# A transformer layer on one core: sums spread over the second sweep, and a written order for the passage into the second FFN

## The chip, the core and the metric

The kernel runs on one core of a Trainium2 chip. The core has five engines that run side by side and wait for each other through semaphores: TensorE (PE; its weight loads are shown apart as PEld), VectorE (DVE), ScalarE (ACT), GpSimd (POOL) and SyncE (SP), whose queue issues nearly all transfers here. TensorE writes to PSUM; the other data lies in SBUF or in the chip's main memory. The metric is the device time of one execution in microseconds (us), taken as the median of the runs.

## The reference, cut to what matters

One layer on 512 tokens of width 1024, all in float32. The weights are of the sizes in the comments.

```python
def swiglu(u, w_in, w_out):                      # w_in 1024 x 5632, w_out 2816 x 1024
    a, b = jnp.split(u @ w_in, 2, axis=-1)
    return (jax.nn.silu(a) * b) @ w_out

sh1, sc1, g1, sh2, sc2, g2, sh3, sc3, g3 = split(silu(c) @ w_ada + b_ada, 9)
u = rms_norm(x, ffn1_norm_g) * (1 + sc1) + sh1
x = x + 0.5 * g1 * swiglu(u, ffn1_w_in, ffn1_w_out)
u = rms_norm(x, mix_norm_g) * (1 + sc2) + sh2
z = u @ w_mix + b_mix                            # the mixer: an mLSTM branch and an attention branch
...
merged = sigmoid(g_a) * (y_a @ w_branch_a) + sigmoid(g_b) * (y_b @ w_branch_b)
x = x + g2 * (merged @ w_out)                    # w_out 1024 x 1024
u = rms_norm(x, ffn2_norm_g) * (1 + sc3) + sh3
x = x + 0.5 * g3 * swiglu(u, ffn2_w_in, ffn2_w_out)
```

## The kernel before, in words

**Products.** To keep float32 accuracy with the faster reduced format (`F32R`), each operand is split in a high half (`wh`, `uh`, `mh`, a rounded copy, made by ScalarE) and a low half (`wl`, `ul`, `ml`, what remains, made by VectorE as source minus copy). A product is three matmuls (`mm3`, lines 127 to 129): high by high, and each high by the other's low. A 512 KB piece of a weight goes through three steps: a transfer into one of three raw buffers (`raw`, line 92), the copy (line 102) and the subtraction (line 104), into one of four pairs of buffers `wh`, `wl`. The subtraction frees the raw buffer, TensorE's last use frees the pair.

**Order.** Each engine works through its instructions in a fixed order. A planner draws it up when the kernel is built, from a cost model: it takes what is ready by that model, what stands first in the program first. An instruction that is pinned (`keep_in_program_order`) stays behind the instruction of its engine that comes before it in the program. `self.pin` is either that function or one that does nothing (`self.free`). Later instructions that are not pinned may still be put between pinned ones. Transfers on the sync queue are issued in the planner's order, each after its waits.

**Output products of the two FFNs** (`pair_out`, from line 526). The 22 blocks of the hidden width are taken in 11 pairs, and the four 256-token by 512-column quarters of the output come from seven block products in place of eight, with sums of weights (`ws`, prepared earlier and kept in main memory) and of activations (`A1`, `A2`). The first sweep over the pairs makes three of the products (Z, X, Y); from them come P1, U2 and U4, each for two blocks of 128 tokens. The second sweep makes the other four (Z, Y, X, W, of two token blocks each, eight PSUM banks) in 8 iterations of 24 matmuls, two raw loads an iteration (`prepare`: c, the plain weights, and d, the sums). The last three iterations (the tail) are done bank by bank in the order X, Z, Y, W (`close`), so that sums and stores can run behind them. In iterations 3, 5 and 7 the d of a tail iteration is loaded ahead (`early`); in iterations 3 to 6 a block of x is loaded. At iterations 6 and 7, P1, U2 and U4 are multiplied by the gate g (`scaled`, line 597) and added to x (`onto`, line 600), seven operations an iteration. In the first FFN the tail is handed to `end` (written out in `run`, all pinned), which goes over into the mixer; the second FFN ends the kernel, with stores at line 607.

**Passage into the second FFN.** `token_gemm` (line 650) multiplies the merged branches with `w_out`: for each half of the columns, four PSUM banks (one for each block of 128 tokens), the weights in four pieces, the first piece for all blocks, the last three block by block. `done` (from `residual`) multiplies the bank by the gate, adds it to x and has ScalarE take the squares and their sum (`x_sq`). In the second column half, ahead of block 3's last pieces, `norm_half(0)` norms blocks 0 and 1: `xnorm` (a chain of small VectorE operations, then xn on VectorE and ScalarE), `norm_turn` (16 transposes on TensorE into four banks) and `norm_u` (for each k of 8: `uh` on ScalarE, `uf` on VectorE, and `ul`, the difference, on VectorE for even k and GpSimd for odd k, line 267). `norm_half(1)` does blocks 2 and 3 behind block 3. `ffn_in_halves` then makes the first two column tiles of both halves of `w_in` (four weight tiles) in halves of 256 tokens, tile after tile, with SiLU and product behind each pair. None of it is pinned. Then `ffn_in` takes the other 20 tiles, in 512-column matmuls, while weight sums for the output product are loaded (`sa`, `sb`) and made.

Of the kernel before, what the change touches and what calls it, by code (L numbers as in the profile page):

```python
# [11 lines left out]
F32 = mybir.dt.float32  # L12
# [35 lines left out]
class Layer:  # L48
# [209 lines left out]
    def u_from(self, ps, k, c0, w, G, sh, pool):  # L258

        nc = self.nc  # L260
        uf = self.tmp(pool, "uf")
        nc.scalar.activation(self.uh[k][:, c0:c0 + w], ps, AF.Identity, scale=G, bias=sh)
        if self.uf_act:
            nc.scalar.activation(uf[:, :w], ps, AF.Identity, scale=G, bias=sh)
        else:
            nc.vector.tensor_scalar(uf[:, :w], ps, G, sh, op0=MUL, op1=ADD)
        (nc.gpsimd if k % 2 else nc.vector).tensor_tensor(  # L267
            self.ul[k][:, c0:c0 + w], uf[:, :w], self.uh[k][:, c0:c0 + w], op=SUB)

# [12 lines left out]
    def norm_half(self, hf, pool, G, sh):  # L282

        xn = self.xnorm(hf, pool)
        self.norm_u(hf, self.norm_turn(hf, xn), pool, G, sh)

# [11 lines left out]

    def norm_u(self, hf, b, pool, G, sh):
        for k in range(NK):  # L300
            self.u_from(b[k // 2][:, k % 2 * 256:(k % 2 + 1) * 256], k, hf * 256, 256, G[:, k:k + 1], sh[:, k:k + 1], pool)
# [109 lines left out]

    def ffn_in_halves(self, w_in, nj, hp, tp):

        wa = [self.w_stat(w_in, j * P) for j in range(nj)]
        wb = [self.w_stat(w_in, FF + j * P) for j in range(nj)]
        pp = [(self.gbank(), self.gbank()) for _ in range(nj)]
        for h in range(2):
            for j in range(nj):
                c0, c1 = h * 256, (h + 1) * 256
                self.gemm_stat(pp[j][0], wa[j], c0, c1)  # L420
                self.gemm_stat(pp[j][1], wb[j], c0, c1)
                self.pair_h(self.pair_s(pp[j][0], c0, c1, tp), pp[j][1], j, c0, c1, hp, tp)


# [102 lines left out]
    def pair_out(self, w, v, hp, tp, x_src, end=None):  # L527
# [7 lines left out]
        def two(*src):  # L535

            n = 2 // len(src)
            t = self.raw(sh, [(lambda t, i=i: t[:, i:i + n, :] if n > 1 else t[:, i, :], a) for i, a in enumerate(src)])
            return self.split(t, sh)
        def early(src, n):  # L540

            hi, lo = [hp.tile(sh, F32R, name=self.nm("we"), tag=f"A{n + i}", bufs=1) for i in range(2)]
            t = lo.bitcast(F32)
            nc.sync.dma_start(t, src)
            nc.scalar.activation(hi, t, AF.Copy)
            V(lo, t, hi, op=SUB)
            return hi, lo
# [60 lines left out]
        tail, ds = 3, []  # L608
        for i in range(NP - tail):
# [39 lines left out]

    def token_gemm(self, lhs, nk, w, half, done, tail=2, extra=None, last=None):  # L650
# [18 lines left out]
        for tb in range(NT):  # L669
            if last and tb == NT - 1:  # L670
                last()
# [4 lines left out]
    def residual(self, factor, v, half, tp, final=False):  # L676
# [3 lines left out]
        def done(tb, half, ps):  # L680
            s = slice(half * 512, (half + 1) * 512)
            t = self.tmp(tp, "rs")
            nc.vector.scalar_tensor_tensor(t, ps, factor, g, op0=MUL, op1=MUL)
            x = self.x[tb][half]
            nc.vector.tensor_tensor(x, x, t, op=ADD)
            if not final:
                self.x_sq(tb, half, t)
            else:
                nc.sync.dma_start(self.out[0, tb * P:(tb + 1) * P, s], x)
# [592 lines left out]
    def run(self):  # L1282
# [7 lines left out]
        self.ntmp, self.xn_tiles, self.gb_tag, self.uf_act = 4, self.xn_ffn, ("gb", 2), True  # L1290
# [130 lines left out]
        self.uf_act = False  # L1421
# [75 lines left out]
        with tc.tile_pool(name="br", bufs=1) as bp:  # L1497
# [30 lines left out]
            def x_spill(h):  # L1528
                for tb in range(NT):
# [10 lines left out]
        with tc.tile_pool(name="f2t", bufs=1) as tp, tc.tile_pool(name="f2h", bufs=1) as hp:  # L1540
# [3 lines left out]
            self.ffn_in_halves(A["ffn2_w_in"][0], 2, hp, tp)  # L1544
# [44 lines left out]
```

## Time and profile before

| | |
|---|---|
| median of 3 runs | 1325.62 us (1324.99 to 1326.6) |
| the profiled execution | 1324.8 us |
| its span, first to last instruction | 1323.0 us |
| TensorE busy in the span | 1304.9 us (99%) |
| VectorE / ScalarE / GpSimd busy | 958.1 / 624.2 / 43.7 us |
| granted TensorE clock, mean | 0.999 |

The profile is of one execution. Its page gives the busy time of each engine; further views list who waited for whom, the instructions in order of time, and the busy time in given windows. Times in them count from the start of the span. A row of a timeline reads: start, duration, engine, line and operation, the tile written, the tiles read, the shape, and in brackets the engine's idle time before it with what ended it. A busy TensorE is not one at its peak, because matmuls overlap: a gap is read from the distance between starts.

### The profile page before, as it was taken

How to read it: one execution, taken by the hardware profiler on the slowest of the kernel's cores; microseconds unless marked ns; L12 is line 12 of the kernel's file. 1: busy time of each engine (PE TensorE's matmuls, PEld its weight loads, DVE VectorE, ACT ScalarE, POOL GpSimd, SP SyncE). 2: the span in 40 equal slices, each digit the busy share in tenths (PEclk: the TensorE clock that was granted, in tenths of full speed). 3: DMA queues.
4: the chain of work that ended last, by engine and by line, in shares of the span. 5: the costliest groups of instructions: out<-in, count | busy, mean ns of one | idle time of the engine just before them, and what ended most of it. 6: DMA issues, size and time to landing. Idle time of an engine off the chain costs nothing.

```text
span 1323.0 us, 17767 instructions
## 1 busy us (share of the span) xinstructions
PE 1304.9 (99%) x6332; PEld 1091.7 (83%) x6332; DVE 958.1 (72%) x1740; ACT 624.2 (47%) x1038; POOL 43.7 (3%) x65
## 2 busy tenths in 40 slices
PE   7999999999999999999999999999999999999998
PEld 6788888888799888888888788878888888888886
DVE  6877777477788687887877778777577656635777
ACT  5633233355476555566566666334262223223742
POOL 1000000000010101000000000003010000000000
PEclk9999999999999999999999999999999999999999
DMA  9999978465845434533243536777439777624574
GB/s 289 272 327 306 309 251 298 133 195 170 293 118 145 120 104 133 151 104 117 83 120 88 159 98 205 225 245 227 162 97 332 273 233 276 208 96 142 169 260 153
DMA packets 204344, 254.18 MB, mean 192 GB/s; under 512 B 14992, under 2 KB 146480, under 8 KB 204256
## 3 DMA queue, kind: packets, MB, share of 16 engines
q1 hardware_dynamic: 203872, 252.98, 60.0%
q8 instruction: 50, 0.82, 0.3%
q14 instruction: 38, 0.31, 0.1%
q0 software_dynamic: 320, 0.06, 0.0%
q10 hardware_dynamic: 64, 0.02, 0.0%
HBM read 217.28 MB, written 35.72 MB: 191 GB/s over the span
## 4 chain that ended last, share of the span: by engine, by line
PE 89%; DVE 4%; DMA 3%; ACT 2%; issue 1%; SPq 0%; POOL 0%; DVEq 0%; ACTq 0%; POOLq 0%
PE g L129 23%; PE g L127 23%; PE g L128 23%; PE t L128 4%; PE t L129 4%; PE t L127 4%; PE g L825 2%; PE t L1208 1%; PE t L1178 1%; DVE wl L104 1%; DMA x<-x_d 1%; PE t L1149 1%; PE t L825 1%; DMA raw<-in_ffn_w_out_dram 1%; PE t L1150 1%
## 5 line engine op out<-in xcount | busy, mean ns | idle before, releaser
L102 ACT ACTIVATE wh<-raw 128x1024 fp32r<-128x1024 f32 (+2 forms) x250 | 254.2, 1019 | 380.6 <-DMA raw<-in_ffn_w_in_dram 106.4
L104 DVE TENSOR_TENSOR wl<-raw,wh 128x1024 fp32r<-128x1024 f32 (+2 forms) x250 | 293.0, 1174 | 179.3 <-ACT wh L102 155.5
L128 PE MATMUL g<-ul,wh 128*128 128x512 f32 (+1 forms) x912 | 348.1, 383 | 1.1 <-POOL ul L267 1.1
L127 PE MATMUL g<-uh,wh 128*128 128x512 f32 (+1 forms) x912 | 348.7, 384 | 0.0
L129 PE MATMUL g<-uh,wl 128*128 128x512 f32 (+1 forms) x912 | 348.3, 382 | 0.0
L128 PEld LDWEIGHTS g<-ul,wh 128*128 128x128 f32 x912 | 171.3, 188 | 34.5 <-POOL ul L267 1.9
L129 PEld LDWEIGHTS g<-uh,wl 128*128 128x128 f32 x912 | 171.5, 188 | 33.6
L127 PEld LDWEIGHTS g<-uh,wh 128*128 128x128 f32 x912 | 171.0, 188 | 32.5 <-issue 0.6
L325 DVE SCALAR_TENSOR_TENSOR acc<-raw,ccol,acc 128x512 f32<-128x512 f32 (+1 forms) x70 | 66.8, 975 | 43.6 <-DMA raw<-in_w_ada_dram 43.5
L127 PE MATMUL g<-wh,uh 128*128 128x512 f32 (+1 forms) x256 | 97.4, 381 | 0.0
L129 PE MATMUL g<-wh,ul 128*128 128x512 f32 (+1 forms) x256 | 96.6, 378 | 0.0
L128 PE MATMUL g<-wl,uh 128*128 128x512 f32 (+1 forms) x256 | 96.4, 377 | 0.0
L128 PE MATMUL t<-wl,A 128*128 128x512 f32 x176 | 69.0, 392 | 1.7 <-DVE wl L104 1.7
L127 PE MATMUL t<-wh,A 128*128 128x512 f32 x176 | 68.6, 390 | 0.0
L129 PEld LDWEIGHTS g<-wh,ul 128*128 128x128 f32 x256 | 48.1, 188 | 9.0
L127 PEld LDWEIGHTS g<-wh,uh 128*128 128x128 f32 x256 | 48.2, 188 | 8.7 <-DVE tk L1046 0.5
L128 PEld LDWEIGHTS g<-wl,uh 128*128 128x128 f32 x256 | 48.2, 188 | 8.3
L129 PE MATMUL g<-yh,wl 128*128 128x512 f32 x128 | 50.1, 392 | 0.3 <-DVE wl L104 0.3
L127 PE MATMUL g<-yh,wh 128*128 128x512 f32 x128 | 49.8, 389 | 0.0
L128 PE MATMUL g<-yl,wh 128*128 128x512 f32 x128 | 49.8, 389 | 0.0
L455 ACT ACTIVATE A<-E 128x768 fp32r<-128x768 f32 x22 | 18.6, 846 | 57.0 <-DVE E L454 51.1
L1160 ACT ACTIVATE S<-S,mn 128x128 f32<-128x128 f32 (+1 forms) x64 | 35.6, 558 | 16.0 <-DVE mn L1152 9.9
(343 smaller groups left out, 2185.2 us busy)
## 6 DMA issues: line engine op xcount, KB each, us to landing
raw<-in_ffn_w_in_dram SPq DMA_DIRECT2D x82, 512.0 KB, 5.1
raw<-in_w_ada_dram SPq DMA_DIRECT2D x56, 512.0 KB, 5.5
raw<-in_w_mix_dram SPq DMA_DIRECT2D x46, 512.0 KB, 4.5
sa<-in_ffn_w_out_dram SPq DMA_DIRECT2D x22, 512.0 KB, 5.9
sb<-in_ffn_w_out_dram SPq DMA_DIRECT2D x44, 256.0 KB, 5.9
ws<-sa SPq DMA_DIRECT2D x22, 512.0 KB, 3.9
ws<-sb SPq DMA_DIRECT2D x44, 256.0 KB, 4.2
raw<-ws SPq DMA_DIRECT2D x44, 256.0 KB, 3.5
```

The lines of the kernel that those rows point to most:

```text
L102: nc.scalar.activation(hi, src, AF.Copy)
L104: self.last_lo = nc.vector.tensor_tensor(lo, src, hi, op=SUB)
L127: pin(mm(ps, lh, rh, start=start, stop=False))
L128: pin(mm(ps, lh, rl, start=False, stop=False))
L129: self.last_mm = pin(mm(ps, ll, rh, start=False, stop=stop))
L325: nc.vector.scalar_tensor_tensor(a, r[:, s], c, a, op0=MUL, op1=ADD)
L455: nc.scalar.activation(A1[:, 0:3, :], E[:, 0:3, :], AF.Copy)
L825: pin(nc.tensor.matmul(acc_ps[b], (wl if p == 1 else wh)[:, b % 2, s], self.ul[k] if p == 2 else self.uh[k], start=k == 0 and p == 0, stop ...
L1149: nc.tensor.matmul(ps[:, :w], q[:, s], k[:, :w], start=True, stop=False)
L1150: nc.tensor.matmul(ps[:, :w], q[:, s], kl[:, :w], start=False, stop=True)
L1160: nc.scalar.activation(S[:, ws], S[:, ws], AF.Exp, scale=-1.0, bias=m, accum_out=sm[:, qb:qb + 1])
L1178: tr = lambda b, c, qb, kb: nc.tensor.transpose(b[:, c:c + P], S[:, P_OFF[qb] + kb * P:P_OFF[qb] + (kb + 1) * P], self.ident)
```

## The change

In `pair_out` the three scalings of P1, U2 and U4 are done in place at iterations 0, 1 and 2 of the second sweep, and the additions to x, one block of tokens an iteration, at 4 to 7. In odd iterations the d weights are loaded into a tile of the tag `xn` in place of a raw buffer (`two_x`). In the second FFN the bank W of token block 1 is closed after iteration 7 and added to x; its last three iterations go into two new banks of 256 columns, each scaled, added and stored by itself.

The passage into the second FFN becomes one function, `passage`, that pins every engine's order. The second column half of the output product is the same, but the transposes stand behind the first three matmuls of block 3's last pieces. The weights of the first four FFN tiles are loaded and split in it, tiles 1 and 2 in two halves each into tiles of the tag `yl`. Both copies of u (`uh` and `uf`) are ScalarE's, and all subtractions VectorE's. TensorE takes tiles 0 and 1 together, k by k, then tile 2, the transposes of the second half, tile 3, and the second half in the same order. SiLU and product follow on whole 512-column banks. `norm_half`, `norm_u`, `u_from`, `ffn_in_halves` and `uf_act` are gone.

```diff
+        def two_x(src):
+            t = tp.tile(sh, F32, name=self.nm("raw"), tag="xn", bufs=1)
+            nc.sync.dma_start(t, src)
+            return self.split(t, sh)
...
-        banks = {"Z": Z, "Y": Y, "X": X, "W": W}
+        banks, tail = {"Z": Z, "Y": Y, "X": X, "W": W}, 3
         def prepare(i, d=None):
             c = two(both(2 * i + 1))
-            d = d or two(self.ws[i][:, 1:3, :])
+            d = d or (two_x if i % 2 else two)(self.ws[i][:, 1:3, :])
             A2 = self.A2[i]
             a = lambda n: (A2[0][:, n, :], A2[1 + n // 2][:, n % 2, :])
             b = lambda n: ((c, d)[n // 2][0][:, n % 2, :], (c, d)[n // 2][1][:, n % 2, :])
             return {"Z": (a(0), b(0)), "Y": (a(3), b(1)), "X": (a(2), b(2)), "W": (a(1), b(3))}
-        step = lambda n, tb, i, o: mm(banks[n], tb, *o[n], i == 0, i == NP - 1)
+        step = lambda n, tb, i, o: mm(banks[n], tb, *o[n], i == 0, i == NP - (1 if end or n != "W" or not tb else 1 + tail))
...
-        tail, ds = 3, []
+        ds = []
         for i in range(NP - tail):
...
-            if i in (6, 7):
-                tb = i - 6
-                add(P1[tb], 0, (tb,))
-                add(U2[tb], 0, (tb + 2,))
-                add(U4[tb], 1, (tb, tb + 2))
+            for src, half in ((P1, 0), (U2, 0), (U4, 1))[i:i + 1]:
+                for tb in range(2):
+                    scaled(src[tb], half, src[tb])
+            if i >= 4:
+                tb = i - 4
+                onto(tb, 0, (P1, U2)[tb // 2][tb % 2])
+                onto(tb, 1, U4[tb % 2])
...
+        add(W[1], 0, (3,))
         for n in "XZYW":
             for tb in range(2):
+                if n == "W" and tb:
+                    for c in (slice(0, 256), slice(256, 512)):
+                        ps, x, r = self.gbank((P, 256)), self.x[3][0][:, c], slice(P, 2 * P)
+                        for i, o in enumerate(os):
+                            a, b = o[n]
+                            self.mm3(ps, a[0][:, r], a[1][:, r], b[0][:, c], b[1][:, c], i == 0, i == tail - 1)
+                        t = self.tmp(tp, "rs")[:, :256]
+                        nc.vector.scalar_tensor_tensor(t, ps, 0.5, g[0][:, c], op0=MUL, op1=MUL)
+                        V(x, x, t, op=ADD)
+                        nc.sync.dma_start(self.out[0, 3 * P:4 * P, c], x)
+                    continue
...
+    def passage(self, lhs, w_out, w_in, bp, G, sh):
+
+        nc, tc = self.nc, self.tc
+        pin = tc.keep_in_program_order
+        done = self.residual(0.5, 5, 1, bp)
+        ps = [self.gbank() for _ in range(NT)]
+        def step(tb, ch, wc, k2s=(0, 1)):
+            for k2 in k2s:
+                k = 2 * ch + k2
+                lh, ll = lhs(k)
+                self.mm3(ps[tb], lh[:, tb * P:(tb + 1) * P], ll[:, tb * P:(tb + 1) * P],
+                         wc[0][:, k2, :], wc[1][:, k2, :], k == 0, k == NK - 1)
+        cols = (0, FF, P, FF + P)
+        ws = {}
+        def load(m):
+            return self.raw([P, NK, P], [(lambda t: t, w_in[:, cols[m]:cols[m] + P].rearrange("(k p) n -> p k n", p=P))])
+        def apart(m):
+            r = load(m)
+            half = lambda n: [bp.tile([P, 4, P], F32R, name=self.nm(n), tag="yl", bufs=8) for _ in range(2)]
+            hi, lo = half("fh"), half("fl")
+            for i in range(2):
+                pin(nc.scalar.activation(hi[i], r[:, 4 * i:4 * i + 4], AF.Copy))
+            ws[m] = lambda k: (hi[k // 4][:, k % 4, :], lo[k // 4][:, k % 4, :])
+            def rest():
+                for i in range(2):
+                    pin(nc.vector.tensor_tensor(lo[i], r[:, 4 * i:4 * i + 4], hi[i], op=SUB))
+            return rest
+        def whole(m):
+            r = load(m)
+            hi = self.wp.tile([P, NK, P], F32R, name=self.nm("wh"), tag="wh", bufs=4)
+            lo = self.wp.tile([P, NK, P], F32R, name=self.nm("wl"), tag="wl", bufs=4)
+            ws[m] = lambda k: (hi[:, k, :], lo[:, k, :])
+            return (lambda: pin(nc.scalar.activation(hi, r, AF.Copy)),
+                    lambda: pin(nc.vector.tensor_tensor(lo, r, hi, op=SUB)))
+        wc = self.w_mov(w_out, 0, 512)
+        for tb in range(NT):
+            step(tb, 0, wc)
+        wcs = [self.w_mov(w_out, ch * 256, 512) for ch in range(1, 4)]
+        self.pin = pin
+        for f in whole(0):
+            f()
+        lo1 = apart(1)
+        lo1()
+        def close(tb):
+            for i, wc in enumerate(wcs):
+                step(tb, 1 + i, wc)
+        close(0)
+        lo2 = apart(2)
+        done(0, 1, ps[0])
+        lo2()
+        close(1)
+        done(1, 1, ps[1])
+        close(2)
+        xn = self.xnorm(0, bp)
+        step(3, 1, wcs[0], (0,))
+        b = self.norm_turn(0, xn)
+        step(3, 1, wcs[0], (1,))
+        step(3, 2, wcs[1])
+        step(3, 3, wcs[2])
+        def part(hf, b, k, act):
+            self.u_part(hf, b, k, bp, G, sh, act, nc.vector)()
+        t = done(2, 1, ps[2], False)
+        part(0, b, 0, True)
+        self.x_sq(2, 1, t)
+        for k in range(1, 5):
+            part(0, b, k, True)
+        hi3, lo3 = whole(3)
+        t = done(3, 1, ps[3], False)
+        part(0, b, 5, True)
+        part(0, b, 6, True)
+        self.x_sq(3, 1, t)
+        part(0, b, 7, True)
+        xn = self.xnorm(1, bp)
+        pp = [self.gbank() for _ in range(4)]
+        def first(h, ms):
+            c = slice(h * 256, (h + 1) * 256)
+            for k in range(NK):
+                for m in ms:
+                    self.mm3(pp[m][:, c], *ws[m](k), self.uh[k][:, c], self.ul[k][:, c], k == 0, k == NK - 1)
+        first(0, (0, 1))
+        hi3()
+        lo3()
+        first(0, (2,))
+        b = self.norm_turn(1, xn)
+        first(0, (3,))
+        for k in range(NK):
+            part(1, b, k, True)
+        first(1, (0, 1))
+        first(1, (2,))
+        first(1, (3,))
+        self.pin = self.free
+        return pp
+
...
             x_spill(0)
             G3, sh3 = self.mod_cols(6, gain(R_N3), self.mod_load(6), self.tbank)
-            self.token_gemm(lhs, NK, A["w_out"][0], 1, self.residual(0.5, 5, 1, bp), 3, None,
-                            lambda: self.norm_half(0, bp, G3, sh3))
-            self.norm_half(1, bp, G3, sh3)
+            pp = self.passage(lhs, A["w_out"][0], A["ffn2_w_in"][0], bp, G3, sh3)
...
-            self.ffn_in_halves(A["ffn2_w_in"][0], 2, hp, tp)
+            for j in range(2):
+                self.pair_h(self.pair_s(pp[2 * j], 0, T, tp), pp[2 * j + 1], j, 0, T, hp, tp)
```

More of the change, by code (lines that the diff above doesn't have):

```diff
@@ L648, in pair_out, with token_gemm @@
                     store(q, half)
-    def token_gemm(self, lhs, nk, w, half, done, tail=2, extra=None, last=None):
+    def token_gemm(self, lhs, nk, w, half, done, tail=2, extra=None):
         nch = nk // 2
@@ L678, in residual, with done @@
+    def residual(self, factor, v, half, tp):
         nc = self.nc
         g = self.mod_bcast(v, half, tp)
-        def done(tb, half, ps):
-            s = slice(half * 512, (half + 1) * 512)
+        def done(tb, half, ps, square=True):
             t = self.tmp(tp, "rs")
-            nc.vector.scalar_tensor_tensor(t, ps, factor, g, op0=MUL, op1=MUL)
+            self.pin(nc.vector.scalar_tensor_tensor(t, ps, factor, g, op0=MUL, op1=MUL))
             x = self.x[tb][half]
-            nc.vector.tensor_tensor(x, x, t, op=ADD)
-            if not final:
+            self.pin(nc.vector.tensor_tensor(x, x, t, op=ADD))
+            if square:
@@ L687, in done @@
                 self.x_sq(tb, half, t)
-            else:
-                nc.sync.dma_start(self.out[0, tb * P:(tb + 1) * P, s], x)
+            return t
         return done
```

32 lines of the change are left out of this document (1 added, 31 removed).

## The prediction

> **What bounds the kernel now.** I read the page first, then the chain and the waits of TensorE, then timelines of each engine around every wait. The page says that TensorE sets the time:
>
> ```profile
> PE 1304.9 (99%) x6332; PEld 1091.7 (83%) x6332; DVE 958.1 (72%) x1740; ACT 624.2 (47%) x1038; POOL 43.7 (3%) x65
> ```
>
> The change alters no product, so it can only fill gaps of TensorE. In the list of waits two groups lie where the diff works:
>
> ```profile
> PE t L128 <- DVE wl L104: 1.7, 3, 0.7
> PE g L128 <- POOL ul L267: 1.1, 3, 0.5
> ```
>
> The first are weights of the FFN output products (`pair_out`, second sweep), late on VectorE; the second is the low half of u, made by GpSimd in `norm_half` before the second FFN. The rest of the list belongs to code that is not changed.
>
> A wait costs more than its bracket, as TensorE's timeline shows (start, duration, line, tiles, in brackets the idle time before):
>
> ```profile
> 960.05 0.39 PE L129 MATMUL g<-wh,ml 128*128 128x512 f32 x1
> 960.28 0.39 PE L127 MATMUL g<-wh,mh 128*128 128x512 f32 x1
> ...
> 966.68 0.28 PE L127 MATMUL g<-uh,wh 128*128 128x256 f32 x1
> ...
> 967.75 0.28 PE L127 MATMUL g<-uh,wh 128*128 128x256 f32 x1
> 968.37 0.39 PE L128 MATMUL g<-ul,wh 128*128 128x256 f32 x1 [0.34 <-POOL ul L267]
> ```
>
> A 512-column matmul shows 0.39 us, yet the next starts 0.23 us later; a 256-column one shows 0.28, and 966.68 to 967.75 is nine steps of 0.12. The end is thus shown 0.16 us late, and the first after a wait takes 0.11 more (0.39 for 0.28). So a wait costs its bracket + 0.27.
>
> **Part 1, the second sweep.** The three waits, and the chain of the last one, from the load to the matmul (start, duration, engine, line):
>
> ```profile
> 359.54 0.50 PE L128 MATMUL t<-wl,A 128*128 128x512 f32 x1 [0.65 <-DVE wl L104]
> ...
> 1279.09 0.50 PE L128 MATMUL t<-wl,A 128*128 128x512 f32 x1 [0.39 <-DVE wl L104]
> ...
> 1280.90 0.40 SPq L92 DMA_DIRECT2D raw<-in_ffn_w_out_dram  x1
> ...
> 1287.92 1.06 ACT L102 ACTIVATE wh<-raw 128x1024 fp32r<-128x1024 f32 x1 [2.08 <-DMA raw<-in_ffn_w_out_dram]
> ...
> 1289.63 1.22 DVE L104 TENSOR_TENSOR wl<-raw,wh 128x1024 fp32r<-128x1024 f32 x1
> ...
> 1290.90 0.50 PE L128 MATMUL t<-wl,A 128*128 128x512 f32 x1 [0.63 <-DVE wl L104]
> ```
>
> One wait is the first FFN's: 0.65 + 0.27 = 0.92. Two are the second's: 0.39 + 0.63 + 0.54 = 1.56. In the chain the transfer takes 7.0 us (1280.90 to 1287.92), ScalarE 1.06, and VectorE comes to it 0.65 us late (1289.63 against 1288.98), because sums stand in front. A raw buffer is thus held 7.0 + 1.06 + 0.65 + 1.22 = 9.9 us; an iteration (24 matmuls, 24 x 0.23 = 5.5 us) needs two loads, so three buffers must turn in 8.2 us. They cannot: supply falls behind as soon as transfers are that slow.
>
> The change gives every second iteration's second load (`two_x`) the tile `xn` in place of a raw buffer. Then three buffers carry three loads in two iterations, 10.9 us for each: 9.9 fits. The 14 sums (6 scalings, 8 additions) stay 14 of the same size; the scalings, now in place, stand at iterations 0 to 2, the additions two an iteration at 4 to 7. In the before trace the order is the planner's, and some of them already ran early, so for the sums alone I count only the 0.65 us above, which is in the same wait. I take 1.4 of the second FFN's 1.56 (ends 0 and 1.56), 0.9 of the first's (ends 0 and 0.92).
>
> New costs: in the first FFN `xn` holds the remainders of the last pair until VectorE has split them, so the load for iteration 1 can't start before that.
>
> ```profile
> 314.98 0.69 DVE L482 TENSOR_TENSOR Rb<-R,A 128x512 fp32r<-128x512 f32 x1
> ...
> 316.87 0.33 SPq L92 DMA_DIRECT2D raw<-in_ffn_w_out_dram  x1
> ...
> 320.43 1.06 ACT L102 ACTIVATE wh<-raw 128x1024 fp32r<-128x1024 f32 x1 [4.93 <-DMA raw<-in_ffn_w_out_dram]
> ...
> 321.57 0.39 PE L128 MATMUL g<-wl,A 128*128 128x512 f32 x1
> ```
>
> Free at 314.98 + 0.69 = 315.67; a transfer at this moment takes 3.6 us (316.87 to 320.43), at worst the 7.0 above; then 1.06 and 1.22. So its low half is there at 321.6 to 325.0, and TensorE wants it at 321.57, the second matmul of bank X. Loss 0 to 3.4; the near row is the 3.6 us one, with others in flight behind it: I take 0.4. In front of the split of iteration 1's first weights VectorE now has a scaling more: 0.1 in each FFN (0 to 0.65, the lateness counted above). So: first FFN -0.9 + 0.4 + 0.1 = -0.4; second -1.4 + 0.1 = -1.3.
>
> **Part 2, the end.** Bank W of token block 1 is the last to close. Its first eight iterations are now summed ahead (one multiply and one add on VectorE more, while it waits anyway for products of X), and the last three come in two halves of 256 columns.
>
> ```profile
> 962.96 0.43 DVE L267 TENSOR_TENSOR ul<-uf,uh 128x256 fp32r<-128x256 f32 x1
> ...
> 1318.20 0.69 DVE L597 SCALAR_TENSOR_TENSOR rs<-g,gb 128x512 f32<-128x512 f32 x1 [0.62 <-PE g L129]
> 1318.93 0.69 DVE L600 TENSOR_TENSOR x<-x,rs 128x512 f32<-128x512 f32 x1
> ...
> out_dram<-x SPq DMA_DIRECT2D x8, 256.0 KB, 2.0
> ...
> h_d<-hn SPq DMA_DIRECT2D x16, 128.0 KB, 1.8
> ```
>
> Before: multiply and add end at 1319.62. After: 18 matmuls of 0.12 = 2.16 in place of 9 of 0.227 = 2.04, +0.1; the two operations on 256 columns take about 0.43 each (as the subtraction L267 does) in place of 0.69: -0.5, of which 0.2 is lost because the first half's pair is still running when the second half closes. The last store moves half the bytes: -0.2. Together -0.4 (ends 0 and -0.9, if nothing of the first half is in the way and the store halves).
>
> **Part 3, the passage.** the rest of TensorE's rows, from the transposes behind the first matmul of block 3 (960.28) to the first 512-column product of the second FFN:
>
> ```profile
> 960.79 2.15 PE L295 MATMUL t<-ident,xn 128*128 128x128 f32 x16
> ...
> 962.70 0.47 PE L128 MATMUL g<-wl,mh 128*128 128x512 f32 x1
> ...
> 971.12 0.39 PE L128 MATMUL g<-ul,wh 128*128 128x256 f32 x1 [0.22 <-POOL ul L267]
> ...
> 982.76 0.39 PE L128 MATMUL g<-ul,wh 128*128 128x256 f32 x1 [0.53 <-POOL ul L267]
> ...
> 993.54 0.40 PE L127 MATMUL g<-uh,wh 128*128 128x512 f32 x1
> ```
>
> Before, the transposes end at 962.70 because xn is late; after, they stand behind three matmuls of block 3. They end when they did, and two matmuls fewer follow: -0.45. The three waits are 0.34 + 0.22 + 0.53 + 3 x 0.27 = 1.90. So at most -2.35: the new FFN tiles start at 966.68 - 0.45 = 966.2, and the first 512-column product at 991.2 instead of 993.54.
>
> Does the written order keep TensorE fed? It takes GpSimd out, puts both copies of u on ScalarE (16 in a half, first and last of 16 at 373.00 and 379.93, where the first passage already works so) and the subtraction on VectorE:
>
> ```profile
> 373.00 0.56 ACT L275 ACTIVATE uh<-t,sh,G 128x256 fp32r<-128x256 f32 x1 [1.25 <-PE t L295]
> ...
> 379.93 0.57 ACT L277 ACTIVATE uf<-t,sh,G 128x256 f32<-128x256 f32 x1
> ...
> 958.67 0.16 DVE L247 SCALAR_TENSOR_TENSOR v<-ss 128x2 f32<-128x2 f32 x1 [0.85 <-ACT rs L229]
> ...
> 960.25 1.34 ACT L254 ACTIVATE xn<-x,rq 128x512 f32<-128x512 f32 x2 [1.62 <-DVE rq L154]
> ...
> 961.78 1.02 ACT L262 ACTIVATE uh<-t,sh,G 128x256 fp32r<-128x256 f32 x2 [0.19 <-PE t L295]
> 962.69 0.63 ACT L229 ACTIVATE rs<-x 128x512 f32<-128x512 f32 x1
> ...
> 964.66 1.07 ACT L102 ACTIVATE wh<-raw 128x1024 fp32r<-128x1024 f32 x1
> ```
>
> A copy every 6.93 / 15 = 0.46 us. From 961.78: 16 copies and two squares (7.4 + 1.25) end at 970.4, the last subtraction at 970.9. The square of block 3 is seventh of eight in that row; its sum is ready when block 3 has closed (966.2) plus multiply, add and one subtraction in front, 968.1, before ScalarE reaches it at 968.8. TensorE, with two weight tiles at once, uses 6 x 0.12 = 0.72 us for each k, so wants the eighth at 966.2 + 5.04 = 971.2. Margin 0.3 us, no wait. The next norm chain (958.67 to 960.25, 1.6 us) and xn copies (1.34) end at 970.9 + 2.9 = 973.8; TensorE is in the third tile until 966.2 + 72 x 0.12 = 974.8. The fourth tile's weights follow xn on ScalarE (1.07) and VectorE (1.22): 976.1, while the transposes (1.9, 960.79 to 962.70) end at 976.7. In the second half the copies start near 975 and have 7.4 us, TensorE needs the last near 984.6. Weight tiles 1 and 2 sit in `yl` and leave two weight buffers free, so the first products of the next FFN have theirs early. Banks: the first pair is freed by SiLU and product while TensorE is in tiles three and four of the second half (48 x 0.12 = 5.8 us). Halving tiles 1 and 2 for `yl` costs each engine about 0.2 us a tile (2 x 0.63 for 1.07, 2 x 0.69 for 1.22), before block 1 closes, when both idle; the loads on the sync queue are the same four.
>
> What the trace doesn't show is whether the planner puts a copy of the next FFN's weights, which now has a buffer, into a gap of the pinned row. None: 0. One of 1.07 on ScalarE against a margin of 0.3: 0.8. Two, and one subtraction of 1.22 on VectorE: 3.1. The margin is thin, so I take 0.35: -2.0 (ends -2.35 and +0.8).
>
> **Sum.** -0.4 - 1.3 - 0.4 - 2.0 = -4.1 us. The profiled execution took 1324.8 us, its span 1323.0; the sum makes that 1320.7, and the median of the runs, 0.8 us above the profiled one, 1321.5.
>
> **Rivals.**
> *ScalarE sets the passage* (foreign copies in the pinned rows). For: two weight buffers and their loads are free by then, and the planner fills any gap it sees. Against: the row from 373.00 to 379.93 has no foreign copy, though there no buffer was free. It costs 0.8 to 3.1 in place of 0.35: 1322.0 to 1324.3.
> *Bandwidth, not buffers, bounds the sweep*, so that `two_x` doesn't do what it says. The table of windows (length, busy times, granted clock, share of the DMA engines, GB/s), iteration 0 and iteration 5 of the second FFN:
>
> ```profile
> 1256.60:1262.00 5.40, 5.40 (x26) 4.46 (x25) 5.40 (x8) 2.20 (x4) 0.00 (x0) 1.00 0.13 34
> ...
> 1284.40:1289.90 5.50, 5.50 (x26) 4.51 (x25) 5.06 (x7) 2.80 (x3) 0.00 (x0) 1.00 1.04 397
> ```
>
> With weights (1.05 MB), x (0.52) and half an early load (0.26) an iteration moves 1.84 MB, 335 GB/s, against 397 measured when full, and iteration 0 leaves the engines idle, where a fourth buffer can load ahead. So 84% at the busiest: not bound. If it is, part 1 gains nothing and keeps its 0.6 of costs: +0.6 - 0.4 - 2.0 = -1.8, 1323.8. The Trainium skill (DMA: Bandwidth & Descriptors, section Bandwidth) puts the limit of HBM transfers at about 358 GB/s for a core; by that the busy iterations would stand at 94%, and this rival would be the likelier. The 397 of the window is above that figure, and the measurement decides.
> *Slower: the sync queue.* It issues in order, and once the passage is over it is held by loads for the weight sums (`sa`) that wait for its memory:
>
> ```profile
> SPq L499 <- POOL ul L267: 7.3, 1, 7.3
> ```
>
> Now that memory may be the `yl` tiles, read until the third tile of the second half has ended: 966.2 + 168 x 0.12 + 1.9 = 988.3. If the planner puts `sa` ahead of the first load of the next FFN, that one starts at 988.3 behind 1.05 MB (2.6 us at 397 GB/s) and needs 7.0 + 1.06 + 1.22 = 9.3 more: 1000.2, against the 991.2 at which TensorE wants it. 9 us lost: 1330.5, slower. It decides as soon as that load stands behind `sa`. Against: its raw buffer is free before block 2 closes, 28 us earlier.
>
> **Chances.** Forecast 0.55, own range 1319.8 to 1322.9; ScalarE 0.17 (half of it still faster by over 0.2%); bandwidth 0.14; the queue 0.09; 0.05 for planner shifts elsewhere, 0.01 of it slower. 0.2% is 2.65 us, about what a measurement of this kernel can tell from no change: below 1322.97 is faster, above 1328.3 slower. Faster 0.66, within 0.24, slower 0.10. All good ends together (-0.92 - 1.56 - 0.9 - 2.35 = -5.7) give 1319.9, and 0.4 is allowed for a row that is hidden in another; low 1319.5. High: ScalarE's worst with 1.7 of the late first load (half of its 3.4): 1326.
>
> **What would show it.** Right: no wait on L104 in the second sweeps above 0.2 us, no ul wait between 960 and 995, transposes behind three matmuls of block 3, 512-column products of the second FFN some 2 us earlier after the transposes; last store after two 128x256 pairs. Wrong: a wait of bank X on its weights at the first FFN's iteration 1; `wh` copies with line 102 between the copies of u; a bracket on the third or fourth tile; waits of the second sweep with raw loads still at 7 us and more.

## The result, and the profile after

The changed kernel takes 1320.05 us (median of 6 runs, 1318.79 to 1320.41) against 1325.93 us for the kernel before beside it: ratio 0.9956, 95% interval 0.9946 to 0.9967. In a later set of runs (after_again) the same kernel took 1320.94 against 1325.21: 0.9965 (0.9953 to 0.9978). So it is faster by 0.2 to 0.5%. The prediction was 1321.5 us (1319.5 to 1326), 4.1 less than before; the medians give 5.9 less in the first set and 4.3 in the later one. The profiled execution took 1320.06 us (span 1318.2), 4.7 less than the one before.

The page of the changed kernel: busy times, then the chain by engine.

```profile
PE 1303.2 (99%) x6341; PEld 1092.7 (83%) x6341; DVE 955.4 (72%) x1736; ACT 629.6 (48%) x1054; POOL 36.9 (3%) x57
...
PE 93%; DVE 3%; ACT 2%; DMA 1%; issue 1%; ACTq 0%; DVEq 0%
```

TensorE's waits (total us, times, longest): the row `PE t L128 <- DVE wl L104` of the output products is gone, and of the three waits for `ul` one is left, now for VectorE.

```profile
PE g L897 <- ACT uh L844: 2.6, 2, 1.4
PE t L1250 <- DVE fq L1200: 0.5, 2, 0.3
PE g L128 <- DVE ul L268: 0.4, 1, 0.4
```

For the comparison of kernels I cut the span at three starts of TensorE: the first matmul of the passage's second column half, the first 512-column product of the second FFN, and the first matmul of the last bank. In the changed kernel's timeline they are:

```profile
941.56 0.50 PE L127 MATMUL g<-wh,mh 128*128 128x512 f32 x1
...
990.88 0.40 PE L127 MATMUL g<-uh,wh 128*128 128x512 f32 x1
...
1311.92 0.28 PE L127 MATMUL g<-we,A 128*128 128x256 f32 x1
```

The lengths of the four stretches, in one profiled execution of each kernel (before: cuts at 942.44, 993.54 and 1315.96; the spans in the traces are 1322.99 before and 1318.25 after, which the page rounds). "Sweep 1" is the time by which the distances between TensorE's starts from 300 to 365 us exceed the steps of 0.227 us; it is a part of the first stretch.

| kernel | to the passage | passage | second FFN | end | sweep 1 |
|---|---|---|---|---|---|
| before | 942.4 | 51.10 | 322.42 | 7.02 | 1.34 |
| changed | 941.6 | 49.32 | 321.04 | 6.32 | 0.43 |
| after_again | 941.8 | 49.19 | 321.05 | 6.32 | 0.51 |
| sweep_only | 941.2 | 51.08 | 321.05 | 6.33 | 0.43 |
| passage_only | 943.0 | 49.45 | 322.60 | 7.02 | 1.99 |
| no_xn | 942.2 | 49.83 | 322.25 | 6.32 | 2.03 |
| xn_alone | 942.3 | 51.09 | 320.82 | 7.03 | 0.41 |
| ada_behind | 942.2 | 48.62 | 321.05 | 6.32 | 0.89 |
| w_whole | 942.2 | 49.66 | 321.05 | 7.02 | 1.12 |
| turn_first | 943.5 | 49.71 | 321.06 | 6.32 | 1.35 |
| pool_odd | 942.5 | 49.61 | 321.05 | 6.33 | 0.82 |
| mended | 940.9 | 48.64 | 321.05 | 6.32 | 0.20 |
| mended_thirds | 943.6 | 48.62 | 321.05 | 6.65 | 0.21 |
| sums_late | 941.9 | 48.62 | 320.86 | 6.32 | 0.36 |

The last three stretches repeat to within 0.1 us wherever the code in them is the same (the passage to 0.6, for a reason shown below). The first does not: changed, after_again, sweep_only, ada_behind, w_whole, turn_first and pool_odd have the same order of instructions up to there and lie between 941.2 and 943.5. A difference of one or two microseconds in it proves nothing. Much of it is in code that no run edits: the start of the kernel (its first matmuls differ by up to 0.9 us between the runs), and one wait for a weight of the mixer near 881 us, with a bracket of 0.15 in the changed kernel and 1.26 in turn_first. Before to changed: -0.9 there, -1.78 in the passage, -1.38 in the second FFN, -0.70 at the end, -4.7 in all. The -0.9 is what the first FFN's sweep gained (1.34 to 0.43); outside the sweep the changed kernel lost 0.6 before 25 us and gained as much after the sweep, no more than runs with the same order differ by.

### The profile page after: what moved, and what is told of

It is laid out like the page before. It is cut to its first block, busy times and chain, and to the rows that moved or that the text cites. A ratio compares the mean times of both kernels' runs of the same rounds, so it can differ in the third digit from the quotient of the medians.

```text
span 1318.2 us, 17786 instructions
## 1 busy us (share of the span) xinstructions
PE 1303.2 (99%) x6341; PEld 1092.7 (83%) x6341; DVE 955.4 (72%) x1736; ACT 629.6 (48%) x1054; POOL 36.9 (3%) x57
## 4 chain that ended last, share of the span: by engine, by line
PE 93%; DVE 3%; ACT 2%; DMA 1%; issue 1%; ACTq 0%; DVEq 0%
PE g L129 23%; PE g L127 23%; PE g L128 23%; PE t L127 4%; PE t L129 4%; PE t L128 4%; PE g L897 2%; PE t L1280 1%; PE t L1250 1%; PE t L1221 1%; PE t L897 1%; PE t L1222 1%; PE t L797 1%; ACT uh L263 0%; DVE wl L104 0%
## 5 line engine op out<-in xcount | busy, mean ns | idle before, releaser
L102 ACT ACTIVATE wh<-raw 128x1024 fp32r<-128x1024 f32 (+2 forms) x246 | 249.3, 1017 | 373.6 <-PE g L128 128.7
L104 DVE TENSOR_TENSOR wl<-raw,wh 128x1024 fp32r<-128x1024 f32 (+2 forms) x246 | 287.6, 1172 | 160.1 <-ACT wh L102 135.6
L127 PE MATMUL g<-uh,wh 128*128 128x512 f32 (+1 forms) x880 | 341.0, 388 | 0.0
L128 PE MATMUL g<-ul,wh 128*128 128x512 f32 (+1 forms) x880 | 339.5, 386 | 0.4 <-DVE ul L268 0.4
L129 PE MATMUL g<-uh,wl 128*128 128x512 f32 (+1 forms) x880 | 339.6, 386 | 0.0
L129 PEld LDWEIGHTS g<-uh,wl 128*128 128x128 f32 x880 | 165.3, 188 | 33.6
L128 PEld LDWEIGHTS g<-ul,wh 128*128 128x128 f32 x880 | 165.4, 188 | 33.0 <-DVE ul L268 0.6
L127 PEld LDWEIGHTS g<-uh,wh 128*128 128x128 f32 x880 | 165.3, 188 | 32.8 <-issue 0.6
L128 PE MATMUL g<-wl,uh 128*128 128x512 f32 (+1 forms) x256 | 96.4, 377 | 0.0
L128 PE MATMUL t<-wl,A 128*128 128x512 f32 x176 | 68.5, 389 | 0.0
L128 PEld LDWEIGHTS g<-wl,uh 128*128 128x128 f32 x256 | 48.2, 188 | 8.3
L128 PE MATMUL g<-yl,wh 128*128 128x512 f32 x128 | 49.8, 389 | 0.0
```

The lines of the kernel that those rows point to most:

```text
L102: nc.scalar.activation(hi, src, AF.Copy)
L104: self.last_lo = nc.vector.tensor_tensor(lo, src, hi, op=SUB)
L127: pin(mm(ps, lh, rh, start=start, stop=False))
L128: pin(mm(ps, lh, rl, start=False, stop=False))
L129: self.last_mm = pin(mm(ps, ll, rh, start=False, stop=stop))
```

## The experiments

**The two parts, each alone.** `sweep_only` is the changed `pair_out` in the kernel before, `passage_only` the old `pair_out` in the changed kernel.

> The output products of the changed kernel (both FFNs) with the passage of the kernel before. Theory: the parts add up, so the gaps of TensorE go in the first FFN's second sweep (0.9 us), in the second FFN's (1.4) and at the end (0.8), and the passage from 942 to 993 stays at 51.1 us: 3.0 us less, about 1322.9. The 0.9 us that the changed kernel saves between 400 and 800 us, where nothing was changed, comes too if it follows from the end of the first FFN (1322.0). Rival: the gain hangs on both parts together, then this kernel and the one with the passage alone do not add up to the 4.4 to 7.2 us measured for the whole change.

> The passage of the changed kernel with the output products of the kernel before. Theory: only the passage shortens, by 1.8 us (51.1 to 49.3), with the one wait on ul at the second half's first tile that the changed kernel shows; the waits on L104 in both second sweeps stay at about 0.65, 0.39 and 0.63 us: about 1323.9. Rival: the faster passage moves loads of the second FFN so that its second sweep runs without the waits as well; then 1322.5.

Measured: sweep_only 1321.53 us (ratio 0.9973, 0.9965 to 0.9982), passage_only 1323.06 (0.9988, 0.9979 to 0.9996). Against 1325.27 beside them that is -3.7 and -2.2 us, together 5.9, as the whole change in its first set of runs (4.3 in the later one, so the medians alone don't show that the parts add up). The table does: each part changes its own stretches and leaves the other's as they were. The waits of the second sweep do not go by a faster passage.

**Buffers or sums.** `no_xn` takes the fourth place for loads away, `xn_alone` adds only that to the kernel before.

```diff
-            d = d or (two_x if i % 2 else two)(self.ws[i][:, 1:3, :])
+            d = d or two(self.ws[i][:, 1:3, :])
```

> The changed kernel with every second sweep's loads in the three raw buffers again (no load into the tile xn); the sums stay spread. Theory of the prediction (buffers bound the sweep): three loads in 8.2 us cannot be had with buffers held 9.9 us, so waits on L104 come back in both second sweeps, some 0.9 us in the first FFN and 1.3 in the second: about 1322.3. Rival (the sums in front of the splits were the cause): no wait comes back, 1320.0. Rival (bandwidth): nothing changes either, and raw loads take 6 us and more as in the changed kernel.

> The kernel before with one edit: every second load of sums in the second sweeps goes into the tile xn. The fourteen sums stay at iterations 6 and 7, end and passage as before. Theory of the prediction (buffers): the waits on L104 go, 0.9 + 1.4 us: about 1323.3. Rival (the sums in front of the splits): the waits of the second FFN stay, at least 0.65 us each, since the additions still stand in front of the splits at iterations 6 and 7: 1324.7.

Measured: no_xn 1321.62 us (0.9973, 0.9964 to 0.9982), xn_alone 1322.88 (0.9982, 0.9973 to 0.9991). TensorE's row for these weights in no_xn's list of waits, which xn_alone's does not have, and one of the waits in its timeline:

```profile
PE t L128 <- DVE wl L104: 1.8, 3, 0.8
```

```profile
1287.94 0.50 PE L127 MATMUL t<-wh,A 128*128 128x512 f32 x1
1289.20 0.50 PE L128 MATMUL t<-wl,A 128*128 128x512 f32 x1 [0.76 <-DVE wl L104]
...
1277.16 1.22 DVE L104 TENSOR_TENSOR wl<-raw,wh 128x1024 fp32r<-128x1024 f32 x1
1278.58 0.49 SPq L92 DMA_DIRECT2D raw<-in_ffn_w_out_dram  x1
1287.92 1.23 DVE L104 TENSOR_TENSOR wl<-raw,wh 128x1024 fp32r<-128x1024 f32 x1 [0.60 <-ACT wh L102]
```

So it is the buffers: with `xn` alone all three waits go (0.41 us at iteration 1 of the first FFN is left, for the late load that the prediction priced), with the sums spread alone one of the second FFN's two stays (it costs 1.1 us) and the first FFN's get no shorter. The three rows behind the dots are the chain of the wait that stays: the load goes out 0.2 us behind the end of the subtraction that frees its buffer, and by the time its own subtraction can start, VectorE has been idle for 0.60 us. No sum stands in front of it. The spread sums even cost 0.2 us in the second FFN: 320.82 without, 321.05 with them. The cost is in iteration 0, where the split of the weights now stands behind two sums (VectorE, then TensorE, changed kernel):

```profile
1252.11 1.37 DVE L542 TENSOR_TENSOR U<-g,P 128x512 f32<-128x512 f32 x2
1253.40 1.22 DVE L104 TENSOR_TENSOR wl<-raw,wh 128x1024 fp32r<-128x1024 f32 x1
...
1254.34 0.39 PE L127 MATMUL t<-wh,A 128*128 128x512 f32 x1
1254.67 0.50 PE L128 MATMUL g<-wl,A 128*128 128x512 f32 x1
```

1254.34 to 1254.67 is 0.33 for a step of 0.227, and the first matmul after it takes 0.11 more. Bandwidth does not bound the sweep either: xn_alone moves the same bytes as before, without the waits. The table of windows of the changed kernel, for the two iterations that the prediction shows (they start 2.7 and 3.1 us earlier here):

```profile
1253.90:1259.30 5.40, 5.40 (x24) 4.22 (x23) 5.40 (x9) 3.12 (x5) 0.00 (x0) 1.00 0.28 101
1281.30:1286.80 5.50, 5.50 (x26) 4.54 (x25) 4.53 (x6) 1.99 (x3) 0.00 (x0) 1.00 0.91 327
```

101 GB/s in place of 34 in iteration 0, 327 in place of 397 in iteration 5: the transfers start earlier and the peak is lower. The limit of about 358 GB/s that the Trainium skill gives (DMA: Bandwidth & Descriptors, section Bandwidth), which that section also calls a core's part when both cores of a pair stream, was passed by the 397 of before; it set nothing here.

**The wait that is left in the passage.** TensorE in the changed kernel, and VectorE at the same time:

```profile
981.56 0.28 PE L127 MATMUL g<-uh,wh 128*128 128x256 f32 x1
982.26 0.39 PE L128 MATMUL g<-ul,wh 128*128 128x256 f32 x1 [0.43 <-DVE ul L268]
...
979.40 0.43 DVE L268 TENSOR_TENSOR ul<-uf,uh 128x256 fp32r<-128x256 f32 x1 [0.48 <-ACT uf L265]
981.12 0.75 DVE L302 TENSOR_SCALAR acc<-raw,ccol 128x1024 f32<-128x1024 f32 x1 [1.29 <-DMA raw<-in_w_ada_dram]
981.79 1.09 DVE L268 TENSOR_TENSOR ul<-uf,uh 128x256 fp32r<-128x256 f32 x3
```

Line 302 is the first operation of a row of w_ada, which the second FFN prepares. It is not pinned, and the planner put it between the pinned subtractions of u. There VectorE waits 1.29 us for a load, and three subtractions behind it are late. It is issued after `self.last_ul`, which in the passage is still a subtraction of the mixer's u. In `ada_behind` that is the last subtraction of the passage:

```diff
-            self.u_part(hf, b, k, bp, G, sh, act, nc.vector)()
+            return self.u_part(hf, b, k, bp, G, sh, act, nc.vector)()
...
-            part(1, b, k, True)
+            self.last_ul = part(1, b, k, True)
```

> The changed kernel with one edit: the first operation of the last weight row of w_ada on VectorE, which stands between the subtractions of u of the second half and waits for its load, must come behind the last of these subtractions. Theory: the gap of TensorE at 982 us (0.69 us, the one wait that is left in the passage) goes, the passage takes 48.6 us in place of 49.3: 1319.4 us. Rival: another row or the copies of the next weights on ScalarE set the subtractions' time, and the gap only changes its name: 1320.0. The loads of w_ada now hold a raw buffer longer; if the next FFN weights wait for it, a wait on L104 or L102 shows up after 985 us and the time is above 1320.

```profile
980.98 0.42 DVE L268 TENSOR_TENSOR ul<-uf,uh 128x256 fp32r<-128x256 f32 x1 [0.49 <-ACT uf L265]
...
983.72 0.43 DVE L268 TENSOR_TENSOR ul<-uf,uh 128x256 fp32r<-128x256 f32 x1 [0.49 <-ACT uf L265]
984.07 0.75 DVE L302 TENSOR_SCALAR acc<-raw,ccol 128x1024 f32<-128x1024 f32 x1
```

This is the only instruction of the kernel whose place in its engine's order changed. The subtractions now follow ScalarE's copies without a break, no wait is left in the passage, and it takes 48.62 us. That is 0.6 to 1.2 less than in the five runs that have the changed kernel's passage as it was (changed, after_again, passage_only, no_xn, w_whole). These vary because that load lands at another moment each time: line 302 starts 39.43 to 40.07 us behind the start of the passage, and each time the passage ends 9.76 us after that start. By time this is too small to see: 1320.69 us, 0.9965 (0.9951 to 0.9979), where 1319.4 was expected. The second FFN takes 321.05 us as before, so the next weights do not wait for the raw buffer.

**Terms of the passage.** `turn_first` puts the transposes ahead of the three matmuls, `pool_odd` gives the subtractions for odd k back to GpSimd.

```diff
-        step(3, 1, wcs[0], (0,))
         b = self.norm_turn(0, xn)
-        step(3, 1, wcs[0], (1,))
+        step(3, 1, wcs[0])
```

> The changed kernel with the transposes of the first half in front of the first matmuls of block 3's last pieces in place of behind three of them. Theory: xn is late, so TensorE waits there, 3 matmuls x 0.227 = 0.68 us less work in front of the transposes; xn's wait of up to 0.7 us appears as a gap in front of them, the rest of the passage stays: 1320.4 to 1320.7. Rival: the planner's ready time does not matter and xn is there in time: no change.

> The changed kernel with the subtractions of u for odd k in the passage given back to GpSimd; the order, and both copies on ScalarE, stay. Theory: GpSimd's subtractions take 0.7 us and more against 0.43 on VectorE, but only every second one is its, one every 0.92 us, so they keep up, and only the last of a half (k = 7) ends about 0.5 us later than on VectorE, against a margin of 0.3: one or two gaps of 0.2 to 0.5 us, 1320.4. Rival (GpSimd was what made the passage wait): the three gaps of the kernel before come back, 1.9 us, 1321.9. Rival: GpSimd is not the cause at all, but the planner's order was, 1320.0.

Measured: turn_first 1321.54 us (0.9969, 0.9956 to 0.9981), pool_odd 1321.51 (0.9973, 0.9964 to 0.9983). Both times are about 1 us above the expected ones, which counted from the changed kernel's first set of runs (1320.05); the stretches are what can be compared. In turn_first the transposes wait:

```profile
961.10 0.39 PE L129 MATMUL g<-wh,ml 128*128 128x512 f32 x1
961.84 2.26 PE L278 MATMUL t<-ident,xn 128*128 128x128 f32 x16 [0.35 <-DVE xn L253]
```

The part up to the new FFN's tiles is 24.55 us there, 23.87 in the changed kernel, 24.24 before: 0.68 for three matmuls' place, as expected; the passage as a whole lost less (49.71), because tiles that start later wait less for that late load. In pool_odd TensorE and GpSimd show:

```profile
971.42 0.28 PE L127 MATMUL g<-uh,wh 128*128 128x256 f32 x1
971.96 0.39 PE L128 MATMUL g<-ul,wh 128*128 128x256 f32 x1 [0.26 <-POOL ul L268]
...
971.17 0.73 POOL L268 TENSOR_TENSOR ul<-uf,uh 128x256 fp32r<-128x256 f32 x1 [2.29 <-ACT uf L265]
...
968.14 0.75 POOL L268 TENSOR_TENSOR ul<-uf,uh 128x256 fp32r<-128x256 f32 x1 [1.09 <-ACT uf L265]
968.24 1.19 DVE L758 TENSOR_TENSOR x<-x,rs 128x512 f32<-128x512 f32 x1
969.46 0.63 ACT L229 ACTIVATE rs<-x 128x512 f32<-128x512 f32 x1 [0.49 <-DVE x L758]
```

One wait on GpSimd, for k = 7 of the first half, 0.42 us with the longer first matmul (the late load of w_ada costs its part in the second half as before). The three waits of before (1.9 us) don't come back. They came less from GpSimd alone than from what stood around it: with both copies on ScalarE and all of it pinned, an engine that takes 0.73 us for every second k keeps up except at the end. No run separates the order from the copies' move to ScalarE. The last three rows show that GpSimd costs more than its own longer subtraction: VectorE's addition of block 3 takes 1.19 us while a subtraction runs on GpSimd, 0.69 in the changed kernel. ScalarE waits for it, and k = 7 starts 0.5 us later.

**The end.** `w_whole` closes the last bank in one piece.

```diff
-                    for c in (slice(0, 256), slice(256, 512)):
+                    for c in (slice(0, 512),):
```

> The changed kernel with the last bank (W of token block 1) closed in one piece of 512 columns, its first eight iterations still summed ahead. Theory: the halves are what shortens the end, so the two operations on VectorE take 0.69 us each again and the store 256 KB: from the first matmul of that bank to the end of the span 7.0 us in place of 6.3, 0.7 more than the changed kernel: 1320.7. Rival: the end is shorter for another reason (the sums ahead), then 6.3 stays.

Measured 1322.56 us (0.9977, 0.9968 to 0.9986), 1.9 above the expected 1320.7, of which the end explains 0.7; the end is 7.02 us, that of before. So the halves make the whole 0.7, the sum ahead by itself nothing. VectorE's last operations in the changed kernel:

```profile
1313.46 0.42 DVE L619 SCALAR_TENSOR_TENSOR rs<-g,gb 128x256 f32<-128x256 f32 x1
1313.91 0.43 DVE L620 TENSOR_TENSOR x<-x,rs 128x256 f32<-128x256 f32 x1
1314.27 0.42 DVE L619 SCALAR_TENSOR_TENSOR rs<-g,gb 128x256 f32<-128x256 f32 x1
1314.73 0.42 DVE L620 TENSOR_TENSOR x<-x,rs 128x256 f32<-128x256 f32 x1
```

**A mended version.** Beside a base run of the changed kernel: `mended` has the edit of ada_behind and, in the first FFN, loads iteration 1's d into a raw buffer; `mended_thirds` also closes the last bank in pieces of 256, 128 and 128 columns.

```diff
-            d = d or (two_x if i % 2 else two)(self.ws[i][:, 1:3, :])
+            d = d or (two_x if i % 2 and (i > 1 or not end) else two)(self.ws[i][:, 1:3, :])
```

> The changed kernel without an edit, as the base for the two kernels beside it on the same chip. Theory: its ratio to the kernel before stays within 0.9946 to 0.9967. The passage takes 49.3 to 49.8 us from the first matmul of its second column half to the first 512-column product, and TensorE's gaps from 300 to 330 us sum to between 0.4 and 1.1 us, since the load into xn lands at another moment in each execution.

> The changed kernel with two edits: the first operation of the last row of w_ada comes behind the last subtraction of u, and in the first FFN the load of iteration 1 goes into a raw buffer, not into xn, which is still occupied by the remainders of the last pair. Theory: the passage takes 48.6 us (0.7 to 1.2 less), and the gap at iteration 1 of the first FFN's second sweep goes, 0.2 to 0.9 us, while the other waits on L104 do not come back, because three raw buffers that start free are enough for the first iterations: 1.2 us less than the changed kernel beside it. Rival: with one load less in xn the supply falls behind and a wait on L104 of 0.4 to 0.7 us comes back near 335 or 346 us; then the passage's gain alone is left, 0.8 us.

> The mended kernel with the last bank closed in three pieces of 256, 128 and 128 columns. Theory: each of VectorE's two last operations and the last store have half the bytes again: from halving before, 0.43 us of engines and 0.33 of the store were saved; a second halving saves at most half of it, 0.4, and nine matmuls more cost what a 128-column matmul takes above half of a 256-column one (0.12 us), unknown, at most 9 x 0.06 = 0.5. So -0.4 to +0.2 us against the mended kernel. Rival: the pairs of operations on VectorE queue behind each other (0.43 + 0.43 us for 256 columns against some 0.6 us of matmuls for 128), so nothing is gained.

Measured: after_again 1320.94 us (0.9965, 0.9953 to 0.9978), mended 1320.20 (0.9959, 0.9945 to 0.9972), mended_thirds 1320.64 (0.9964, 0.9952 to 0.9977). Passage and sweep of mended are where they were expected: 48.64 us, sweep 1 at 0.20, no wait on L104 back. The base's passage took 49.19, just under the 49.3 expected at least, so the edit gained 0.55 us there and not 0.7 to 1.2. By time the three can't be told apart. The thirds lose 0.3 us at the end, more than the 0.2 that was expected at worst: eighteen matmuls of 128 columns stand in place of nine of 256, the expectation priced only nine of them, and one takes hardly less than one of 256 (last section).

**The sums back where they were.** `sums_late` is mended with the fourteen sums at iterations 6 and 7.

> The mended kernel with the fourteen sums back at iterations 6 and 7 of the second sweep, each scaled into a temporary tile as in the kernel before. Theory, after the run with xn alone: a fourth place for loads is all that the sweep needs, and the scalings at iterations 0 to 2 only put the splits of the first iteration later. Then the second FFN from its first 512-column product to its last bank takes 320.8 us, as with xn alone, in place of 321.05 in the mended kernel, and TensorE's gaps from 300 to 330 us go from 0.22 to 0.0; about 0.45 us less in all. Rival: with loads in xn only at odd iterations of the later part in the first FFN, sums in front of the splits cost a wait on L104 of 0.3 us or more again, and the kernel is the slower one.

Measured 1319.82 us (0.9956, 0.9941 to 0.9971). The second FFN takes 320.86 us, as expected. In the first FFN the two gaps of 0.1 at iteration 0 go, but one of 0.30 comes at 324 us, so sweep 1 is 0.36, not 0: there both theories hold a part. It is on a par with mended. Against the kernel before beside them the ratios are 0.9956 and 0.9959, those of the changed kernel 0.9956 and 0.9965: no run shows that either is faster than the changed kernel.

## The prediction, step by step

**What bounds the kernel: right.** No product changed, TensorE stayed at 99%, and the gain is gaps.

**Second FFN's sweep: right.** -1.3 forecast, -1.38 measured, by the mechanism given (three buffers that must turn in 8.2 us and are held 9.9); no_xn and xn_alone show it. The 0.65 us by which sums stood in front of the last split were not what TensorE waited for: in no_xn they are gone and that wait is 0.76 us in place of 0.63. That the spread sums cost little by themselves held: 0.2, where the step had 0.1.

**First FFN's sweep: mechanism right, its balance by luck of the execution.** The waits went, and they were more than the 0.9 counted: the sweep loses 1.3 to 2.0 in the three runs with three buffers. The late load of iteration 1 exists. In w_whole, whose order of instructions is the same there as the changed kernel's, it shows at full size:

```profile
321.43 0.39 PE L129 MATMUL t<-wh,Rb 128*128 128x512 f32 x1
322.06 1.20 PE L127 MATMUL g<-wh,A 128*128 128x512 f32 x4 [0.25 <-ACT wh L102]
323.33 0.49 PE L128 MATMUL g<-wl,A 128*128 128x512 f32 x1
```

Three steps took 0.63, 1.27 and 0.33 us for 0.227, 0.91 and 0.227: 0.87 lost. In the profile of the changed kernel the same place lost 0.17, for the load landed 3.8 us after its issue and not 4.5:

```profile
317.00 0.33 SPq L507 DMA_DIRECT2D raw<-ws  x1
...
320.84 3.91 ACT L102 ACTIVATE wh<-raw 128x1024 fp32r<-128x1024 f32 x4 [5.64 <-DMA raw<-ws]
```

The 0.4 taken lies between. What the step didn't see is the `x4`: the planner put four products of high halves ahead of the first low half, 0.68 us of cover. The net term, -0.4, measured -0.9 between the two profiles. But the seven executions of the new order lose 0.43 to 1.35 us, the two of the old 1.34 and 1.99, so one pair of executions can show anything from nothing to -1.6.

**The end: right mechanism, size too small.** -0.4 forecast, -0.70 measured. From the first matmul to the last add it is 3.23 us for 3.66, -0.43 where the step had -0.2: the 0.2 "lost because the first half's pair is still running" did not occur, since the second multiply (1314.27) starts as soon as its last matmul (1313.95 + 0.28) is done. The store and what follows take 3.10 us for 3.37, -0.27 in place of -0.2.

**The passage: right, and the cause of what is missing was the wrong one.** -2.0 forecast, -1.78 in the profile (-1.3 to -1.9 over the five runs). The -0.45 for the transposes measured -0.37. k = 7 was in time: its subtraction ended 0.5 us before TensorE took it up, where the step had a margin of 0.3. The 0.35 for "a foreign copy in pinned rows" stood for the right risk with the wrong instruction. Two copies of the next weights did get into the row, between the halves, and they are still there in ada_behind, which shows no wait: they cost nothing that TensorE felt. What cost 0.69 us was a VectorE operation that waits for a DMA. Without it the passage gains 2.48, so the upper end, -2.35, was close.

**Rivals.** ScalarE did not set the passage, bandwidth did not bound the sweep, and the slower one, the sync queue held by `sa`, did not happen: the loads of the next FFN's weights went out ahead of `sa`, which was issued at 988.19, when the prediction had its memory free at 988.3. The profile's balance is -4.7 against -4.1: the first FFN's sweep gave 0.5 more than its term and the end 0.3, the passage 0.2 less. The three sizes were off and the passage's shortfall hid a part of the other two, so the sum is closer than its terms.

## What to carry to other kernels

When TensorE waits for weights in a steady loop, add up how long one buffer is held (transfer, copy, queue, subtraction) and compare it with the loads that an iteration needs; one more place to load into was worth all of that wait. With that place there, smoothing VectorE's other work did not pay: with the sums put back, the second FFN's sweep was 0.2 us shorter. An order written by hand holds only what is pinned: look in the trace for foreign instructions in the row, and above all for one that waits for a transfer, since everything behind it waits too. Cut the span at fixed points of the bounding engine: here two stretches repeat to 0.1 us, and a third but for one wait, where whole executions differ by one or two.

## What the runs showed of the hardware

A matmul of 128 columns was hardly shorter than one of 256. In mended_thirds the 128-column ones start 0.11 us apart, against 0.12 for 256 columns and 0.227 for 512:

```profile
1314.66 0.27 PE L127 MATMUL g<-we,A 128*128 128x128 f32 x1
1314.77 0.27 PE L128 MATMUL g<-we,A 128*128 128x128 f32 x1
1314.88 0.28 PE L129 MATMUL g<-we,Ra 128*128 128x128 f32 x1
```

The last bank's matmuls took 2.92 us from the first start to the last, 2.03 in mended: the nine more cost 0.9 us of TensorE, and VectorE's shorter operations and the smaller store gave 0.6 of it back.

Two operations of VectorE took longer while GpSimd ran a subtraction: 1.19 us for an addition that takes 0.69, and 1.59 for the split of line 104 that takes 1.22 (kernel before, 967.81 us, beside a GpSimd subtraction from 967.59 to 968.32).
